# Two tile placements and the place of the second per-layer-embedding products, in a kernel of two blocks

## The chip, the core and the metric

The kernel runs on one core of one Trainium2 chip. The metric is the device time of one execution in microseconds (us); less is better. The engines are named as in the profile: PE (matrix products), DVE, ACT and POOL (vector, scalar and general work), SP (it only issues DMAs here). ACT and POOL issue DMAs as well.

## What is computed

Input is one sequence of T = 512 tokens of width D = 1024, all in fp32. Two blocks follow each other. Cut to what the change touches:

```
# first block, its end: mixture of experts and final norm
x = x + gate1 * (concat(gmlp(h), rwkv7(h)) @ w_out)
h = modulate(rmsnorm(x), shift2, scale2)
group = top1(softmax(h @ rg_w + rg_b)); pick = top2(softmax(logits of its 8 experts))
y = sum over the 2 picked of 32 experts: w * ((silu(h @ w_gate[e]) * (h @ w_up[e])) @ w_down[e])
x = rmsnorm(x + gate2 * y) * final_norm_g
# second block, for i in 0, 1
x = layer_norm(alpha * x + mixer_i(x));  x = layer_norm(alpha * x + swiglu(x))
x = x + (p[i] @ w_ple[i]) * sigmoid(x @ w_ple_gate[i] + b[i])
```

The products `p[i] @ w_ple[i]` (a 512x256 by a 256x1024 matrix for each layer i, "ple products" below) depend on inputs alone, so they can run at any time before layer i ends. They are computed ahead, written to DRAM and read back when the layer needs them.

## The kernel before

**Arithmetic.** Every fp32 product is made of three products in a faster format: each operand is split into a high part and a remainder, and PE computes high x high, high x low and low x high (`mm3`, lines L281 to L283; for the experts `lin`, L1281 to L1283). A weight is loaded as it is into a "raw" tile (`load`, L251, issued by SP), then `conv` makes the high part on ACT (`whi`, L259) and the remainder on DVE (`wlo`, L260). A raw tile can be loaded again once its `wlo` is done, and a pair of parts can be written again once the last product that reads it is done.

**Tiles and order.** Tiles come from pools that are stacked in the on-chip memory in the order in which they are opened. A pool that lies where an older one lay has to wait for the readers of the older tiles. Every engine runs its own instructions in a fixed order that a planner sets from the program text, and waits on semaphores where data or a place isn't ready. `weights` (the function) opens for a stage the pools of low parts, then of raw tiles, then of high parts. In the experts a raw tile or a part is 8 KB of each partition (2048 fp32 values, 1 MB in all); there are five raw tiles and two groups of two pairs of parts, used in turn. Counted in bytes of a partition: `moe` opens a pool at 19,840 with the sorted inputs `xsort`, the constants `c2` and small tiles up to 67,968; the low parts follow up to 100,736, the raw tiles up to 141,696, the high parts up to 174,464. What lay there before: the activation parts of the first block's `w_out` products from 56,704 to 89,472 (read until the last of these products), its own weight tiles below 56,704, and tiles that were done earlier above 89,472.

**Start of the experts (`moe`, L1058).** Early loads: the two halves of expert 0's gate weights (`raw0`), and of layer 0's ple products `pT` and `w_ple` (`rawp`), and then up weights. The router follows (L1099 to L1231): normalisation L1099 to L1104 with L322, L323 and L327, choice of experts on DVE, a count of places on PE (L1202) and DVE (L1201, L1204). The normalised tokens are written to DRAM (`h2d`, L1112) and fetched back in the order of the experts by eight gathers on POOL (`sort`, L1256), turned by PE (L1262) and scaled into `xsort` (L1267, L1269). The ple products of layer 0 stand behind the first gather in the text (L1272); their results leave through ACT (`po`, L1054) and an ACT-issued DMA (L1055). Expert 0 starts with L1281 on `x0h`.

**End of the experts.** `down` of expert 31 ends with `ey` on DVE (L1343) and an adding scatter into `yd` in DRAM, issued by POOL (L1344). Then comes a branch (`tc.If`, L1419) over extra blocks of tokens, which isn't taken here; every engine passes it.

**Start of the second block (`second`).** Weights come in raw tiles of 1024 values (four of them; seven pairs of parts). `ple_load` and `ple_in` fetch and convert pT and w_ple of layer 1; `y` tiles are loaded from `yd` by SP (L1515); `group(2048)` and `group(2304)` load the four raw tiles of `w_mix` that the first products need. `stats` squares y on ACT (L1527), and makes 1/sqrt on ACT and POOL (L1528, L314 to L318); `normed` scales y on DVE (L1535), turns it on PE (L1540) and writes and splits x (L1542, L287, L288). The ple products of layer 1 stand in two parts: five of eight column blocks before the first `normed`, three after the second `stats`. Then 192 products of 256 columns each follow ("bc products", four outputs, eight k, two halves, three products each): the first half with k outside, so that the first steps already want two of the four w_mix tiles, the first and the third. Behind them come x's way to DRAM (`xd`, L1567), the convolution (L1583 to L1587) and the w_dt products (from `s_wdr`, L1601).

## Time and profile before

| | us |
|---|---|
| three runs | 2479.7, 2475.49, 2478.95 |
| median | 2478.95 |
| the profiled execution | 2484.5 |
| its span, first to last instruction | 2482.6 |
| PE busy in it | 2390.5 |
| DVE busy | 1618.2 |
| ACT busy | 1135.6 |
| POOL busy | 231.8 |

All rows come from the one profiled execution, 5.5 us above the median of the runs. Between its span and its own time lie 1.9 us. Of the span, 383 to 467 us is the start of the experts, 467 to 1049 us the experts, and 1049 to 1106 us the way from the last expert through the bc products. In a row of the timeline the columns are start, duration, engine (an engine's name with a q is its queue of issues), line, operation, output<-inputs, shape and count; brackets at the end give the time that the engine stood idle just before, and what it waited for.

### The profile page before, as it was taken

The numbers are of one execution on the slowest core, as the hardware profiler recorded it, in microseconds if no ns is written. First come the engines' busy times: TensorE is split into PE (matmuls) and PEld (weight loads), VectorE is DVE, ScalarE is ACT, GpSimd is POOL, SyncE is SP. The second block draws the span as 40 slices with busy tenths as digits, with TensorE's granted clock in tenths as the row PEclk, the third lists the DMA queues.
The fourth block names the chain that finished last, engine by engine and source line by source line (L and its number), as shares of the span: only waits on it lengthen the run. The fifth ranks groups of instructions, "written<-read, shape, count | busy, mean of one in ns | idle before, by whom it ended". The sixth has DMA issues, their size and how long they took to land.

```text
span 2482.6 us, 36164 instructions
## 1 busy us (share of the span) xinstructions
PE 2390.5 (96%) x14570; PEld 1872.2 (75%) x14570; DVE 1618.2 (65%) x2543; ACT 1135.6 (46%) x1452; POOL 231.8 (9%) x73
## 2 busy tenths in 40 slices
PE   7999999799999999889999999999999998999998
PEld 3788677576666666568878898888888678888887
DVE  4778775699999999866766473333394677333346
ACT  2633324577677777564335333232353654223233
POOL 0000000112334444400000000000000000000000
PEclk9999999899999999989999999999999999999999
DMA  7233334799999999672323323322333112323232
GB/s 250 90 108 109 102 101 176 288 353 354 361 359 359 357 356 359 235 242 86 119 80 113 124 94 102 97 91 92 102 107 107 35 35 86 102 85 109 91 98 69
DMA packets 187307, 408.39 MB, mean 164 GB/s; under 512 B 13408, under 2 KB 130704, under 8 KB 162560
## 3 DMA queue, kind: packets, MB, share of 16 engines
q1 hardware_dynamic: 175840, 383.00, 44.2%
q0 software_dynamic: 5536, 10.46, 1.8%
q10 hardware_dynamic: 5760, 12.59, 1.4%
q8 instruction: 115, 1.88, 0.3%
q14 instruction: 56, 0.46, 0.0%
HBM read 389.17 MB, written 25.21 MB: 167 GB/s over the span
## 4 chain that ended last, share of the span: by engine, by line
PE 52%; DMA 17%; DVE 3%; issue 3%; ACT 1%; POOLq 0%; SPq 0%; DVEq 0%; ACTq 0%
PE mm L282 16%; PE mm L281 16%; PE mm L283 16%; DMA yd<-ey,r 15%; PE sc L1969 1%; PE po L1977 1%; PE pt L1946 1%; DMA raw<-in_w_mix_dram 1%; DVE x L1471 1%; DVE wlo L260 1%; DVE x L1472 0%; DMA s_row<-ard 0%; PE aux L1715 0%; DVE x L1473 0%; DVE xl L288 0%
## 5 line engine op out<-in xcount | busy, mean ns | idle before, releaser
L260 DVE TENSOR_TENSOR wlo<-raw,whi 128x1024 fp32r<-128x1024 f32 (+3 forms) x461 | 756.2, 1652 | 259.5 <-ACT whi L259 258.9
L281 PE MATMUL mm<-xh,whi 128*128 128x512 f32 (+1 forms) x2264 | 833.4, 370 | 17.5 <-ACT xh L287 6.8
L259 ACT ACTIVATE whi<-raw 128x1024 fp32r<-128x1024 f32 (+3 forms) x461 | 637.4, 1403 | 463.2 <-PE mm L282 374.7
L282 PE MATMUL mm<-xl,whi 128*128 128x512 f32 (+1 forms) x2264 | 832.7, 368 | 2.1 <-DVE xl L288 1.8
L283 PE MATMUL mm<-xh,wlo 128*128 128x512 f32 (+1 forms) x2264 | 831.2, 368 | 0.6 <-DVE wlo L260 0.6
L281 PEld LDWEIGHTS mm<-xh,whi 128*128 128x128 f32 x2264 | 427.2, 190 | 96.3 <-issue 9.4
L282 PEld LDWEIGHTS mm<-xl,whi 128*128 128x128 f32 x2264 | 430.3, 190 | 72.5 <-DVE xl L288 4.0
L283 PEld LDWEIGHTS mm<-xh,wlo 128*128 128x128 f32 x2264 | 429.7, 190 | 72.5 <-issue 5.2
L1344 POOL DMA_INDIRECT yd<-ey,r x32 | 210.9, 6590 | 380.7 <-DVE ey L1343 375.8
L1283 PE MATMUL mm<-wlo,exh 128*96 128x512 f32 x496 | 198.0, 401 | 12.1 <-DVE wlo L260 12.0
L1281 PE MATMUL mm<-whi,exh 128*96 128x512 f32 x496 | 197.0, 397 | 4.8 <-ACT exh L287 2.7
L1282 PE MATMUL mm<-whi,exl 128*96 128x512 f32 x496 | 195.8, 395 | 0.0
L1841 DVE TENSOR_TENSOR l_h<-l_sg,mm 128x512 f32<-128x512 f32 x44 | 30.2, 688 | 182.6 <-PE mm L283 167.0
L1283 PEld LDWEIGHTS mm<-wlo,exh 128*96 128x96 f32 x496 | 80.4, 162 | 56.9 <-DVE wlo L260 23.3
L1281 PEld LDWEIGHTS mm<-whi,exh 128*96 128x96 f32 x496 | 80.9, 163 | 38.0 <-ACT whi L259 3.0
L1282 PEld LDWEIGHTS mm<-whi,exl 128*96 128x96 f32 x496 | 80.6, 162 | 35.1
L1282 PE MATMUL aux<-whi,ehl 128*96 128x512 f32 x256 | 100.6, 394 | 0.8 <-DVE ehl L288 0.8
L1281 PE MATMUL aux<-whi,ehh 128*96 128x512 f32 x256 | 100.6, 393 | 0.0
L1283 PE MATMUL aux<-wlo,ehh 128*96 128x512 f32 x256 | 98.4, 400 | 0.0
L287 ACT ACTIVATE xh<-l_h 128x512 fp32r<-128x512 f32 x44 | 27.2, 623 | 111.7 <-DVE l_h L1841 111.7
L1840 ACT ACTIVATE l_sg<-mm 128x512 f32<-128x512 f32 x44 | 25.8, 589 | 83.1 <-PE mm L283 83.0
L1282 PEld LDWEIGHTS aux<-whi,ehl 128*96 128x96 f32 x256 | 41.3, 161 | 19.3 <-DVE ehl L288 1.2
(570 smaller groups left out, 2546.4 us busy)
## 6 DMA issues: line engine op xcount, KB each, us to landing
raw<-in_moe_gate_dram SPq DMA_DIRECT2D x64, 1024.0 KB, 7.5
raw<-in_moe_up_dram SPq DMA_DIRECT2D x64, 1024.0 KB, 7.4
raw<-in_moe_down_dram SPq DMA_DIRECT2D x64, 1024.0 KB, 8.6
raw<-in_w_mix_dram SPq DMA_DIRECT2D x44, 512.0 KB, 3.5
raw<-in_w_ffn_gate_dram SPq DMA_DIRECT2D x44, 512.0 KB, 3.5
raw<-in_w_ffn_up_dram SPq DMA_DIRECT2D x44, 512.0 KB, 3.5
raw<-in_w_ffn_down_dram SPq DMA_DIRECT2D x40, 512.0 KB, 3.3
raw<-in_ada_w_dram SPq DMA_DIRECT2D x64, 256.0 KB, 2.7
```

Source lines behind the costliest of these rows:

```text
L259: nc.scalar.activation(hi[:, :m], r[:, :m], AF.Copy)
L260: nc.vector.tensor_tensor(lo[:, :m], r[:, :m], hi[:, :m], op=OP.subtract)
L281: nc.tensor.matmul(ps, h, xh, start=start, stop=False)
L282: nc.tensor.matmul(ps, h, xl, start=False, stop=False)
L283: nc.tensor.matmul(ps, l, xh, start=False, stop=stop)
L287: self.nc.scalar.activation(xh, src, AF.Copy)
L1281: nc.tensor.matmul(ps, xh[:, k, :], wh, start=(k == 0), stop=False)
L1282: nc.tensor.matmul(ps, xl[:, k, :], wh, start=False, stop=False)
L1283: nc.tensor.matmul(ps, xh[:, k, :], wl, start=False, stop=(k == len(ww) - 1))
L1344: nc.gpsimd.indirect_dma_start(out=yd, out_offset=bass.IndirectOffsetOnAxis(ap=yi, axis=0), in_=y, in_offset=None, bounds_check=T - 1, oob ...
L1840: nc.scalar.activation(sg, pp["g", j], AF.Silu)
L1841: V.tensor_tensor(h, sg, pp["u", j], op=OP.mult)
```

## The change

In `weights` the raw tiles' pool is opened first, ahead of the low parts: it takes 67,968 to 108,928, the low parts move up to 108,928 to 141,696, the high parts stay. A new method `only` restricts the parts to one of the two groups. `conv` can work in pieces of a number of columns; `ple_in` and the first gate weights use pieces of 512. In `moe` the tile `grow` is allocated behind `xsort`, so that `c2` and the small tiles lie 4 KB higher. After `down` of expert 31 and ahead of the branch, pT and w_ple of layer 1 are loaded and converted with the parts of group 0; group 1 is left to the extra blocks. Behind the branch all ple products of layer 1 run in one go, and their results go to eight slices of `xsort`, from where they are written out. In `second` the y loads are issued by POOL, x's tile is allocated behind the y tiles and the statistics' tiles, each half of the statistics has tiles of its own, and the mean and 1/sqrt are made on DVE (and ACT) without POOL.

```diff
     def weights(self, es, raw, hi, lo, wt=WT):
+        self.raw = pool("raw", raw)
         los = [pool("lop", b) for b in lo]
-        self.raw = pool("raw", raw)
         self.groups = [(pool("hip", b), l) for b, l in zip(hi, los)]
         self.hip, self.lop = (sum((g[i] for g in self.groups), []) for i in range(2))
+    def only(self, i):
+        self.hip, self.lop = (list(p) for p in self.groups[i])
...
-    def conv(self, r, kt, n):
+    def conv(self, r, kt, n, step=None):
...
-        nc.scalar.activation(hi[:, :m], r[:, :m], AF.Copy)
-        nc.vector.tensor_tensor(lo[:, :m], r[:, :m], hi[:, :m], op=OP.subtract)
+        for o in range(0, m, step or m):
+            s = slice(o, min(m, o + (step or m)))
+            nc.scalar.activation(hi[:, s], r[:, s], AF.Copy)
+            nc.vector.tensor_tensor(lo[:, s], r[:, s], hi[:, s], op=OP.subtract)
...
-    return K.conv(*raw[0]), sum((K.conv(*r) for r in raw[1:]), [])
-def ple(K, i, ops, bank, room, ms_=range(8)):
+    return K.conv(*raw[0], 512), sum((K.conv(*r, 512) for r in raw[1:]), [])
+def ple(K, i, ops, bank, room):
...
     xsort = mo.tile([128, DC, SLOTS + BLK], F32, name="xsort")
+    grow = mo.tile([128, D], F32, name="grow")
     K.const("c2", mo)
...
     for r in raw0:
-        wg0 += K.conv(*r)
-    grow = mo.tile([128, D], F32, name="grow")
+        wg0 += K.conv(*r, 512)
...
     down(31, *hid, yi[:, 31:], ws[:, 31:])
+    K.only(KEEP)
+    p1 = ple_in(K, ple_load(K, 1))
+    K.only(1 - KEEP)
     total = nc.values_load(nxi[0:1, 0:1], min_val=0, max_val=MORE,
...
     with tc.If(total > 0):
         overflow(total)
+    outs = [xsort[:, m, :T] for m in range(DC)]
+    ple(K, 1, p1, K.mm, lambda: outs.pop(0))
...
-    x = fp.tile([128, DC, T], F32, name="x0")
...
-    p1 = ple_in(K, ple_load(K, 1))
     for b in range(4):
-        nc.sync.dma_start(ys[b], K.yd[b * 128:(b + 1) * 128, :])
+        nc.gpsimd.dma_start(ys[b], K.yd[b * 128:(b + 1) * 128, :])
...
+    nv, nr = ([fp.tile([128, 2], F32, name=f"{n_}{h_}") for h_ in range(2)] for n_ in ("nv", "nr"))
+    sqs = [fp.tile([128, D], BF16, name="sq", bufs=2) for _ in range(4)]
+    x = fp.tile([128, DC, T], F32, name="x0")
...
-        nc.gpsimd.tensor_scalar(v, v, 1.0 / D, 1e-6, op0=OP.mult, op1=OP.add)
-        K.rsqrt(v, r, None, nc.gpsimd)
+        V.tensor_scalar(v, v, 1.0 / D, 1e-6, op0=OP.mult, op1=OP.add)
+        K.rsqrt(v, r)
...
     stats(0)
-    room = lambda: fp.tile([128, T], F32, name="po", bufs=4)
-    ple(K, 1, p1, K.aux, room, range(PM))
     normed(0)
     normed(1)
     stats(1)
-    ple(K, 1, p1, K.aux, room, range(PM, 8))
```

## Rows read from the trace of the kernel before

**Rows 1.** The page's head and its line of PE's busy time (busy us, share of the span, instructions).

```profile
span 2482.6 us, 36164 instructions
PE 2390.5 (96%) x14570; PEld 1872.2 (75%) x14570; DVE 1618.2 (65%) x2543; ACT 1135.6 (46%) x1452; POOL 231.8 (9%) x73
```

**Rows 2.** The view by stretches: stretch in us of the span, its length, busy us and instructions of PE, PE's weight loads, DVE, ACT and POOL, PE's granted clock (1.00 is full), the DMA engines' mean busy share, GB/s. First stretches at the experts' start, then one in their middle, then at their end.

```profile
420.00:425.00 5.00, 2.71 (x20) 2.17 (x19) 5.00 (x8) 2.11 (x7) 0.00 (x0) 1.00 0.50 197
440.00:445.00 5.00, 0.58 (x4) 0.52 (x4) 2.01 (x13) 0.39 (x1) 0.00 (x0) 0.81 1.00 385
445.00:450.00 5.00, 4.74 (x16) 4.26 (x17) 1.50 (x7) 2.00 (x4) 0.00 (x0) 0.50 0.36 136
450.00:455.00 5.00, 5.00 (x27) 4.40 (x27) 3.49 (x21) 0.00 (x0) 2.81 (x3) 0.67 0.60 192
600.00:1000.00 400.00, 387.54 (x1695) 267.76 (x1693) 368.84 (x244) 284.82 (x201) 172.87 (x23) 1.00 0.97 356
1030.00:1040.00 10.00, 10.00 (x47) 7.12 (x46) 8.70 (x6) 6.00 (x4) 3.73 (x1) 1.00 0.09 20
1060.00:1070.00 10.00, 7.11 (x21) 5.50 (x22) 1.93 (x3) 6.93 (x11) 0.97 (x5) 0.61 1.02 363
```

**Rows 3.** The timeline of SP's queue at the experts' start: the first of the early loads, and the constants' load behind them.

```profile
383.58 0.86 SPq L251 DMA_DIRECT2D raw<-in_moe_gate_dram  x2
...
418.23 0.34 SPq L201 DMA_DIRECT2D cst_c<-in_c_dram  x1
```

**Rows 4.** The timeline of DVE at the experts' start: the last eviction of the first block's w_out products, three of the four early `wlo`, and two steps of the router's normalisation.

```profile
419.16 0.75 DVE L902 SCALAR_TENSOR_TENSOR x<-mm,mod,x 128x512 f32<-128x512 f32 x1 [1.96 <-PE mm L283]
419.83 2.28 DVE L260 TENSOR_TENSOR wlo<-raw,whi 128x2048 fp32r<-128x2048 f32 x1
...
423.13 2.29 DVE L260 TENSOR_TENSOR wlo<-raw,whi 128x2048 fp32r<-128x2048 f32 x1
425.33 0.15 DVE L1099 TENSOR_TENSOR n<-sq 128x4 f32<-128x4 f32 x1
...
427.89 2.28 DVE L260 TENSOR_TENSOR wlo<-raw,whi 128x2048 fp32r<-128x2048 f32 x1
430.09 0.15 DVE L327 SCALAR_TENSOR_TENSOR n<-n,n 128x4 f32<-128x4 f32 x1
```

**Rows 5.** The timeline of all engines from the router's end to the first expert.

```profile
441.27 0.58 PE L1202 MATMUL aux<-r,R 128*128 128x8 f32 x4 [1.53 <-DVE r L1198]
...
444.61 0.60 ACT L1054 ACTIVATE po<-mm 128x512 f32<-128x512 f32 x1 [7.45 <-DMA ple<-po]
...
451.58 1.06 POOL L1256 DMA_INDIRECT xt<-h2d,r  x1 [15.14 <-DVE B L1221]
...
466.62 0.65 PE L1281 MATMUL mm<-whi,x0h 128*96 128x512 f32 x1
```

**Rows 6.** The timeline of all engines from the last expert to the bc products (rows of different engines in order of time).

```profile
1048.24 0.39 PE L1283 MATMUL aux<-wlo,ehh 128*96 128x512 f32 x1
1048.67 0.75 DVE L1343 SCALAR_TENSOR_TENSOR ey<-aux,r,grow 96x512 f32<-96x512 f32 x1 [1.09 <-PE aux L1283]
1049.81 0.39 SPq L251 DMA_DIRECT2D raw<-in_pT_dram  x1
...
1051.69 1.42 POOL L1344 DMA_INDIRECT yd<-ey,r  x1 [4.93 <-DMA yd<-ey,r]
...
1056.10 0.79 PE L281 MATMUL aux<-whi 128*128 128x512 f32 x1 [7.47 <-DVE wlo L260]
...
1057.35 2.04 SPq L1515 DMA_DIRECT2D y<-yd  x4
...
1062.89 0.79 PE L281 MATMUL aux<-whi 128*128 128x512 f32 x1 [4.74 <-ACT whi L259]
...
1067.33 0.59 PE L282 MATMUL aux<-wlo,whi 128*128 128x512 f32 x1
...
1069.30 1.42 DVE L1535 TENSOR_SCALAR y<-y,nr 128x1024 f32<-128x1024 f32 x2 [5.20 <-POOL nr L318]
...
1071.43 1.03 PE L1540 MATMUL aux<-cst_c,y 128*128 128x128 f32 x8
```

**Rows 7.** The timeline at the beginning of the bc products (the last two of the four w_mix remainders on DVE, PE's first products) and at their end (PE's last bc product and the first of w_dt).

```profile
1076.14 2.35 DVE L260 TENSOR_TENSOR wlo<-raw,whi 128x1024 fp32r<-128x1024 f32 x2
...
1079.14 0.63 PE L281 MATMUL mm<-xh,whi 128*128 128x256 f32 x4
1080.95 0.39 PE L282 MATMUL mm<-xl,whi 128*128 128x256 f32 x1 [1.18 <-DVE xl L288]
...
1105.21 0.28 PE L283 MATMUL mm<-xh,wlo 128*128 128x256 f32 x1
1106.49 0.41 PE L281 MATMUL mm<-xh,wdh 128*16 128x512 f32 x1 [1.00 <-ACT wdh L287]
```

**Rows 8.** The view of one tile, x, in its stretch: count, duration in ns (min, median, max) of the remainder of 512 columns on DVE.

```profile
L288 DVE TENSOR_TENSOR xl<-x,xh x8: 676/682/684, 1079.0 to 1092.6; 128x512 fp32r<-128x512 f32 x8
```

**Rows 9.** The view of the tile po, which carries the ple results: us from the issue of its DMAs to their landing.

```profile
DMA to landing us min/median/max: 2.0/2.5/9.2
```

**Rows 10.** The view of one line, L1344, the scatter: duration in ns (min, median, max), first and last start in us.

```profile
L1344 POOL DMA_INDIRECT yd<-ey,r x32: 1416/8083/8087, 509.2 to 1051.7; - x32
```

**Rows 11.** The page's list of DMA issues: KB of each, us from issue to landing.

```profile
raw<-in_w_mix_dram SPq DMA_DIRECT2D x44, 512.0 KB, 3.5
```

More of the change, by code (lines that the diff above doesn't have):

```diff
@@ L1024 @@
 RAWR = 2
-PM = 5
+KEEP = 0
 SLOTS = 2 * T
@@ L1040, in ple_in @@
 def ple_in(K, raw):
-    return K.conv(*raw[0]), sum((K.conv(*r) for r in raw[1:]), [])
-def ple(K, i, ops, bank, room, ms_=range(8)):
+    return K.conv(*raw[0], 512), sum((K.conv(*r, 512) for r in raw[1:]), [])
+def ple(K, i, ops, bank, room):
     ps_, wp = ops
-    for m in ms_:
+    for m in range(8):
         ms = slice(m * 128, m * 128 + 128)
@@ L1520, in second @@
     rs = []
+    nv, nr = ([fp.tile([128, 2], F32, name=f"{n_}{h_}") for h_ in range(2)] for n_ in ("nv", "nr"))
+    sqs = [fp.tile([128, D], BF16, name="sq", bufs=2) for _ in range(4)]
+    x = fp.tile([128, DC, T], F32, name="x0")
     def stats(half):
-        v, r = (fp.tile([128, 2], F32, name=n_, bufs=2) for n_ in ("nv", "nr"))
+        v, r = nv[half], nr[half]
         for b in range(2):
-            sq = fp.tile([128, D], BF16, name="sq")
-            nc.scalar.activation(sq, ys[2 * half + b], AF.Square, accum_out=v[:, b:b + 1])
-        nc.gpsimd.tensor_scalar(v, v, 1.0 / D, 1e-6, op0=OP.mult, op1=OP.add)
-        K.rsqrt(v, r, None, nc.gpsimd)
+            nc.scalar.activation(sqs[2 * half + b], ys[2 * half + b], AF.Square, accum_out=v[:, b:b + 1])
+        V.tensor_scalar(v, v, 1.0 / D, 1e-6, op0=OP.mult, op1=OP.add)
+        K.rsqrt(v, r)
         rs.extend((r[:, 0:1], r[:, 1:2]))
```

## The prediction

> **What bounds the kernel now.** I read the views in this order: the head of the page, the stretches, the timelines of the stretches that the change touches, and the rows of single tiles and lines for prices. PE is busy 96% of the span [rows 1], so there is little idle time to win, and the reader's first question is where it lies. In the middle of the experts nothing is to be won: PE is busy 387.5 of 400 us and the DMA engines 0.97 [rows 2], and the change alters nothing there. Two stretches are left, one at each end of the experts.
>
> At the start, PE does 0.58 us of work in 440 to 445 [rows 2], and the first expert begins at 466.62 [rows 5]. What ends last is the router's chain on DVE, then the count on PE, then the gathers (first one issued at 451.58 [rows 5]). Two things stretch this chain. The early `wlo` of 2.28 us each stand between the router's steps [rows 4]. And ACT waits 7.45 us for the DMA of an earlier ple result before it can empty a bank [rows 5], with PE's queue behind it, while the DMA engines are full (share 1.00 [rows 2]). The early raw loads are issued at 383.58, yet the first `wlo` comes at 419.83, right behind the eviction of the last w_out product (419.16, 0.75 us) [rows 3, 4]: the low parts' place is what it waits for. The constants go out only at 418.23 [rows 3] for the same reason.
>
> At the end, the last expert product starts at 1048.24, PE's next is one of layer 1's ple products at 1056.10, and they run on steadily only from 1062.89 [rows 6], because pT and w_ple are asked for at 1049.81, behind the branch. The clock has fallen by then: the granted clock in 1060 to 1070 is 0.61 on average [rows 2]. From 1062.89 to 1067.33 there are eleven products at 0.44 us each [rows 6], the rate of the lower level of 1.2 GHz; in the experts a product takes 387.54/1695 = 0.229 us at full clock, 2.4 GHz [rows 2]. Meanwhile y is fetched (1057.35) and scaled at 1069.30 after a wait for POOL [rows 6], and the bc products start at 1079.14 and run on from 1080.95, held by the split of x, with the w_mix remainders only just done (1076.14 + 2.35 = 1078.5) [rows 7].
>
> **The change part by part. End of the experts.** The two loads of layer 1's ple inputs, 1.5 MB, move into a stretch in which the DMA engines are at 0.09 [rows 2]; at 356 GB/s they take 4.2 us: free. Were that cover gone they would cost these 4.2 us at most. Their conversion is six pieces of 512. The parts of group 0 are those of expert 31's last weights, so the bulk waits for PE's last product, 1048.63. DVE is free of `ey` at 1049.42 [rows 6]; a piece is 0.68 us on DVE [rows 8], and ACT runs a piece ahead, and the first column block wants five of six: 1049.4 + 5 x 0.68 = 1052.8. I add no sum for the branch, since PE passes it while DVE works. The 48 products then take 11 x 0.44 + 37 x 0.229 = 13.3 us if the clock falls as before: 1066.1. Ends: 11.0 us if it doesn't fall (1063.8), 21.1 if it stays low (1073.9).
>
> What is late next is a wait that the change adds. The results are kept in `xsort`, at the lowest addresses, and that is where the raw tiles of the second block begin. Their w_mix loads, issued at 1059.44 now [rows 6], must wait until the ple results have been read out. An eviction and issue is some 0.9 us (0.60 [rows 5] and 0.34 for an issue [rows 3]), a landing 2.0 to 9.2, median 2.5 [rows 9]: 1069.5. Queued behind on SP is all of w_mix, and the bc products wait for that. Four tiles of 0.5 MB follow each other at 0.5 MB / 356 GB/s = 1.47 us; the first lands after 3.5 us [rows 11], the third, which the first bc step wants, 2.9 later: 1076.2 with the issues. Its two conversions at 1.2 each (two took 2.35 [rows 7]) end at 1078.6. Before, the stream ran from 1080.95: 2.6 us gained with the six products that can go ahead, against four now.
>
> The other edits there. The y loads on POOL start when the scatter has landed, as now: nothing. 1/sqrt without POOL saves some 0.7 us of y's way, but y and x are then done ahead of the weights, so this covers itself and gives nothing. The second half's transposes (16, at 1.03 us for eight [rows 6]: 2.1 us) can fill the gap before the weights; I take 1.0, ends 0 and 2.1. The w_dt wait of 1.00 us [rows 7] should go, because its tile no longer lies where x's output is still being read: 1.0, ends 0 and 1.0. Against this, PE now has a gap of up to 12 us before the bc products with only transposes in it. After a gap of 7.5 us the clock was low (above); eleven products at 0.44 in place of 0.229 cost 2.3. I take half, 1.2, ends 0 and 2.3. Sum: 2.6 + 1.0 + 1.0 - 1.2 = 3.4 us gained. Upper end: outputs land 2.3 us sooner, 4.9 + 2.1 + 1.0 = 8. Lower end: low clock all the way through the 48 products, 7.8 us later: 2.6 - 7.8 + 1.0 = -4.2.
>
> One rule of the Trainium skill speaks against one of these edits. The page "SBUF — State Buffer", section "SBUF: two separate sides", says that a DMA issued from POOL needs POOL to write its descriptors, that a DVE operation holding their shared port locks it out, and that such DMAs belong on ACT or SP. The trace agrees in direction: the scatters beside DVE's `wlo` take 8.08 us in the median, the last one, with DVE idle, 1.42 [rows 6, 10]. By it four y loads beside DVE would issue up to 4 x (8.08 - 1.42) = 27 us later; I charge nothing, because no DVE work is due between the pieces' end at 1053.5 and y's scaling.
>
> **Start of the experts.** The raw tiles change places with the low parts. So the conversions are free of the w_out products, but now the raw tiles lie where the w_out activations are read until about 419. I expect the first loads (gate 0, pT, w_ple, the first up weights: 4.5 MB, 12.6 us at 356 GB/s) behind the constants at 419.5 instead of 383.58. Their conversions then arrive between 425 and 437 as pieces of 0.68, in the router's chain or in its gaps, in place of `wlo` of 2.28. Without any `wlo` the chain would win about 5 us: 2.2 before L1099 (423.13 to 425.33) and 3.5 of other `wlo` between L1099 and L327, of which 2.28 is the one shown [rows 4]. But 14 pieces cost 9.5 us if all of them land in the chain. So the chain alone lies between 5 gained and 9.5 - 5.7 = 3.8 lost. The other bound is transfers: up to the gathers the DMA engines idle (1 - 0.50) x 5 + (1 - 0.36) x 5 + (1 - 0.60) x 5 = 7.7 us in 420 to 455 [rows 2], which 12.6 us don't fit into: 4.9 us lost if they all stand in front of the gathers. On the other side, fewer ple products stand in front of the count, and the 7.45 us wait of ACT need not come again. Between these I take zero, ends 10 lost (below) and 5 gained. The moved `grow` and the constants' place 4 KB higher: the constants still wait for the same products, nothing.
>
> The total is 3.4 us. The profiled execution lies 5.5 us above the median; a difference is the same from either, so I take it off the median: 2478.95 - 3.4 = 2475.5, rounded 2475.
>
> **The rivals.** *R1, slower: the late loads collide.* The 4.5 MB delay the gathers by 4.9 us, and w_ple comes last, so that two column blocks' more ple products, 12 at 0.44 = 5.3 us, stand on PE between the gathers and expert 0. Together 10.2 lost, less 3.4 at the end: 2478.95 + 6.8 = 2486. It decides from the point where the first gather is issued later than 451.58 + 4.9 = 456.5. For it: the place argument and the full DMA engines in 440 to 445 [rows 2]. Against it: PE has 4.4 us free there, and gathers need only what DVE's short steps give.
>
> *R2: the change doesn't do what it says at the end.* PE's first ple product comes no earlier than now, 1056.1, because the pieces stand behind the branch or the parts: results land at 1072.8, third weights at 1081.9, 0.9 later than now with 1.0 of w_dt gained and the clock's 1.2 lost: 2480. For it: the parts of group 0 are in use until the last product. Against it: six pieces are short.
>
> *R3: both ends gain.* The early conversions leave the router's chain altogether, because the planner puts them into gaps or some raw tiles' places are free early (those above 89,472): 5 + 3.4 = 8.4, 2470.5. For it: pieces fit into DVE's gaps (DVE works 2.01 of 5 us in 440 to 445 [rows 2]). Against it: the gathers may then wait for transfers.
>
> **How the numbers follow.** Forecast 0.42 (2475, itself from 2470 to 2481), R1 0.17 (2486), R2 0.14 (2480), R3 0.22 (2470), other 0.05. A measurement of this kernel can tell about 0.2%, 5.0 us, from no change: faster means below 2474, slower above 2484. Faster: R3, 0.17 of the forecast and 0.03 of others, 0.42. Slower: R1 and 0.03 of the rest, 0.20. Same: 0.38. The range 2466 to 2487 leaves out the best of R3 with a full clock at the end (8 + 5 gained) and the worst of R1.
>
> **What would show it.** Right: pT and w_ple of layer 1 issued by SP before 1040; PE's first ple product of layer 1 within 5 us of its last expert product; the w_mix loads some 10 us behind where they are now, right after the last ple result has landed; bc products about 3 us sooner, held by a `wlo` of w_mix and no longer by x; no wait before w_dt. At the start: gate 0's loads at about 419.5, pieces of `wlo` from 425 on, expert 0 at 466.6 give or take 5. Wrong: first loads still at 384 (then R3), a first gather after 456.5 (R1), y loads of several us each on POOL (the port), or w_mix loads that don't wait for the ple results (then the end gains several us more).

## The result and the profile after

| | before | after |
|---|---|---|
| median of the runs, us | 2477.74 (5 runs) | 2493.1 (5 runs, 2484.54 to 2494.04) |
| ratio after to before | | 1.0056, 95% interval 1.0042 to 1.007 |
| the profiled execution, us | 2484.5 | 2494.04 |

The change costs 0.56%, some 14 us, where 3.4 us of gain were forecast. One of the five runs of after is 8 us faster than the other four. The head of the page of after, answering [rows 1], says that PE's busy time is nearly the same (2390.5 before): of the 9.6 us by which the span grew, 2.2 are busy time and the rest is idle time:

```profile
span 2492.2 us, 36180 instructions
...
PE 2392.7 (96%) x14570; PEld 1876.5 (75%) x14570; DVE 1619.7 (65%) x2564; ACT 1137.1 (46%) x1465; POOL 249.5 (10%) x67
```

The view by stretches of after, with the columns of [rows 2]:

```profile
440.00:445.00 5.00, 4.98 (x27) 4.71 (x25) 4.01 (x21) 0.00 (x0) 1.90 (x2) 0.50 1.04 420
445.00:450.00 5.00, 3.62 (x15) 3.23 (x16) 4.55 (x18) 0.60 (x1) 3.78 (x5) 0.50 0.96 357
450.00:455.00 5.00, 5.00 (x20) 4.19 (x19) 3.14 (x9) 1.66 (x3) 2.68 (x3) 0.73 1.00 408
...
460.00:465.00 5.00, 1.27 (x3) 1.08 (x4) 0.56 (x1) 1.33 (x2) 0.00 (x0) 0.79 1.02 411
465.00:470.00 5.00, 5.00 (x15) 3.86 (x15) 0.39 (x1) 2.37 (x3) 0.00 (x0) 0.53 0.45 175
470.00:475.00 5.00, 5.00 (x23) 3.48 (x22) 2.91 (x2) 3.77 (x5) 0.00 (x0) 1.00 0.43 116
...
600.00:1000.00 400.00, 388.13 (x1698) 268.45 (x1697) 370.35 (x247) 283.09 (x200) 180.54 (x23) 1.00 0.98 357
```

The middle of the experts is unchanged (last line, against 387.54 in [rows 2]). At the start the picture has turned round. PE is busy in 440 to 445, where it had 0.58 us of work, but at 0.50 of its clock; the DMA engines, which had room in 445 to 455 (0.36, 0.60), are full; and the room has moved to 465 to 475 (0.45, 0.43).

The timeline of after at the experts' start, rows of several engines in order of time, answering [rows 3 to 5]:

```profile
418.73 0.33 SPq L201 DMA_DIRECT2D cst_c<-in_c_dram  x1
419.16 0.85 SPq L255 DMA_DIRECT2D raw<-in_moe_gate_dram  x2
...
422.66 0.16 DVE L1106 TENSOR_TENSOR n<-sq 128x4 f32<-128x4 f32 x1 [0.17 <-ACT sq L1012]
...
442.80 1.03 POOL L1262 DMA_INDIRECT xt<-h2d,r  x1 [12.69 <-DVE B L1228]
...
452.46 20.95 SPq L255 DMA_DIRECT2D raw<-in_moe_up_dram  x2
...
463.07 0.60 ACT L1060 ACTIVATE po<-mm 128x512 f32<-128x512 f32 x1 [5.36 <-DMA ple<-po]
...
463.73 0.79 PE L287 MATMUL mm<-whi 128*128 128x512 f32 x1 [4.11 <-ACT po L1060]
...
469.50 0.58 PE L1287 MATMUL mm<-whi,x0h 128*96 128x512 f32 x1
...
475.71 1.61 PE L1268 MATMUL aux<-cst_c,xt 128*128 128x128 f32 x13
...
492.78 0.47 PE L1287 MATMUL mm<-whi,exh 128*96 128x512 f32 x1 [2.11 <-ACT exh L293]
```

Gate 0's load goes out at 419.16 in place of 383.58. The router is quicker without the large `wlo`: its normalisation starts at 422.66 in place of 425.33, the first gather at 442.80 in place of 451.58. And yet expert 0 begins at 469.50 in place of 466.62. Between them stand an eviction that waits for the DMA of an earlier ple result, twelve ple products at the lower clock (463.73 to 469.0), and on SP's queue a row of 20.95 us, at the end of which the second half of expert 1's up weights is asked for. The last two rows are the turning of gathered rows on PE, which now stands behind expert 0's first product, and the first product of expert 1.

The timeline of after at the experts' end, answering [rows 6, 7]; the last expert product starts at 1053.05:

```profile
1032.86 0.38 SPq L255 DMA_DIRECT2D raw<-in_pT_dram  x1
...
1053.05 0.39 PE L1289 MATMUL aux<-wlo,ehh 128*96 128x512 f32 x1
1053.93 0.50 PE L287 MATMUL mm<-whi 128*128 128x512 f32 x1 [0.49 <-ACT whi L265]
...
1057.06 0.60 ACT L1060 ACTIVATE xsort<-mm 128x512 f32<-128x512 f32 x1 [1.62 <-DVEq L1429]
...
1063.39 2.12 POOL L1524 DMA_DIRECT2D y<-yd  x4 [3.15 <-DMA yd<-ey,r]
...
1067.00 1.06 ACT L1538 ACTIVATE sq<-y 128x1024 bf16<-128x1024 f32 x1 [9.35 <-DMA y<-yd]
...
1068.69 0.80 PE L287 MATMUL mm<-whi 128*128 128x512 f32 x1 [6.39 <-ACT xsort L1060]
...
1075.53 0.60 ACT L1060 ACTIVATE xsort<-mm 128x512 f32<-128x512 f32 x1 [0.79 <-PE mm L289]
...
1076.52 1.28 ACT L326 ACT_TABLE_LOAD   x1 [0.39 <-ACT xsort L1060]
...
1078.29 10.62 SPq L255 DMA_DIRECT2D raw<-in_w_mix_dram  x7
1078.70 1.42 DVE L1546 TENSOR_SCALAR y<-y,nr 128x1024 f32<-128x1024 f32 x2
...
1089.17 0.58 PE L288 MATMUL mm<-xl,whi 128*128 128x256 f32 x1 [1.06 <-DVE xl L294]
...
1115.83 0.40 PE L287 MATMUL mm<-xh,wdh 128*16 128x512 f32 x1
```

The inputs come early and PE's first ple product stands 0.88 us behind the last expert product. But ACT's second eviction stands behind the first square, which waits 9.35 us for y. PE, its four banks full, waits 6.39 us; the last eviction ends at 1076.1, 1/sqrt comes behind it, and w_mix is asked for when the last results have left `xsort`. From the last expert product, y is scaled after 25.65 us (21.06 in [rows 6]), x's low part is first used after 36.12 (32.71 in [rows 7]) and w_dt starts after 62.78 (58.25).

### The profile page after: what moved, and what is told of

It reads as the page before. It is cut to its first block, busy times and chain, and to the rows that moved or that the text cites. A ratio compares the mean times of both kernels' runs of the same rounds, so it can differ in the third digit from the quotient of the medians.

```text
span 2492.2 us, 36180 instructions
## 1 busy us (share of the span) xinstructions
PE 2392.7 (96%) x14570; PEld 1876.5 (75%) x14570; DVE 1619.7 (65%) x2564; ACT 1137.1 (46%) x1465; POOL 249.5 (10%) x67
## 4 chain that ended last, share of the span: by engine, by line
PE 53%; DVE 2%; DMA 1%; ACT 1%; issue 0%; SPq 0%; ACTq 0%; POOLq 0%; DVEq 0%
PE mm L288 16%; PE mm L287 16%; PE mm L289 16%; PE sc L1977 1%; PE po L1985 1%; PE pt L1954 1%; DMA s_row<-ard 0%; DVE x L1483 0%; PE aux L1723 0%; DMA raw<-in_w_mix_dram 0%; PE aux L1725 0%; DMA yd<-ey,r 0%; DVE x L1484 0%; ACT whi L265 0%; DVE wlo L266 0%
## 5 line engine op out<-in xcount | busy, mean ns | idle before, releaser
L1350 POOL DMA_INDIRECT yd<-ey,r x32 | 228.0, 7125 | 377.0 <-DVE ey L1349 361.9
L1849 DVE TENSOR_TENSOR l_h<-l_sg,mm 128x512 f32<-128x512 f32 x44 | 30.1, 687 | 182.5 <-PE mm L289 167.0
L1289 PEld LDWEIGHTS mm<-wlo,exh 128*96 128x96 f32 x496 | 80.6, 162 | 57.2 <-DVE wlo L266 23.8
L1848 ACT ACTIVATE l_sg<-mm 128x512 f32<-128x512 f32 x44 | 25.8, 588 | 83.1 <-PE mm L289 82.9
```

The source lines that it names most:

```text
L1289: nc.tensor.matmul(ps, xh[:, k, :], wl, start=False, stop=(k == len(ww) - 1))
L1350: nc.gpsimd.indirect_dma_start(out=yd, out_offset=bass.IndirectOffsetOnAxis(ap=yi, axis=0), in_=y, in_offset=None, bounds_check=T - 1, oob ...
L1848: nc.scalar.activation(sg, pp["g", j], AF.Silu)
L1849: V.tensor_tensor(h, sg, pp["u", j], op=OP.mult)
```

## The experiments

Two theories, one for each end. *Start*: the raw tiles' new place sends 4.5 MB of loads into a stretch in which the DMA engines are needed for the gathers and the next weights; rivals are the pieces of conversions, the order of the ple products on PE, and the order of conversions. *End*: the evictions on ACT stand in y's way and PE's banks fill; rivals are the results' place, for which w_mix waits, and PE's clock.

All experiments in one table. "Expert 1": from the issue of the constants' load (L201) to the first product of gate and up of expert 1 on DVE. It is the mark for the start, as from there to the same step of expert 31 all nineteen profiles need 530.0 to 534.0 us. "y", "xl" and "w_dt": from the last expert product to y's scaling, the first use of x's low part, and the first w_dt product. The marks come from the one profiled run of each kernel; in e4, s1 and e6 this run lies 9.1, 5.7 and 4.8 us below the median of the timed runs, so there the marks show less than the ratio does.

| kernel | ratio to before, 95% interval | expert 1 | y | xl | w_dt |
|---|---|---|---|---|---|
| before | 1 | 85.6 | 21.1 | 32.7 | 58.3 |
| b1, before again | a single run | 86.8 | 21.0 | 32.5 | 58.8 |
| after | 1.0056, 1.0042 to 1.007 | 91.2 | 25.7 | 36.1 | 62.8 |
| a2, after again | a single run | 91.5 | 25.4 | 35.6 | 62.4 |
| e1, start edits alone | 1.0044, 1.0031 to 1.0057 | 89.8 | 18.9 | 32.5 | 58.2 |
| s1, pools' order alone | 1.0036, 1.0022 to 1.0049 | 90.6 | 19.0 | 32.6 | 58.0 |
| e7, after without the order | 1.0019, 1.0005 to 1.0033 | 86.8 | 25.3 | 35.6 | 62.2 |
| e4, ple behind expert 0 | 1.0097, 1.0084 to 1.011 | 95.7 | 25.8 | 35.3 | 61.0 |
| e8, ple inputs first | 1.0057, 1.0044 to 1.0069 | 91.8 | 25.6 | 35.3 | 61.0 |
| e2, end edits alone | 1.0015, 1.0006 to 1.0023 | 81.9 | 24.7 | 34.9 | 61.5 |
| e6, group 1 for ple | 1.0071, 1.0059 to 1.0083 | 91.8 | 21.8 | 36.0 | 62.4 |
| g1, fewer products | 1.0016, 1.0005 to 1.0026 | 86.5 | 20.2 | 31.4 | 57.9 |
| g2, y from elsewhere | 0.9998, 0.9989 to 1.0007 | 81.9 | 20.7 | 32.5 | 58.0 |
| c1, y loads by POOL | 1.0046, 1.0033 to 1.006 | 80.6 | 30.1 | 39.2 | 65.4 |
| c2, the second block's edits | 0.9998, 0.9989 to 1.0007 | 82.3 | 22.3 | 33.9 | 58.2 |
| d1, e2 and results elsewhere | 1.0044, 1.0031 to 1.0058 | 82.6 | 28.3 | 39.7 | 65.5 |
| d2, d1 and evictions on DVE | 1.0021, 1.0009 to 1.0034 | 82.0 | 22.5 | 34.7 | 61.3 |
| f1, d1 and products ahead | 1.0042, 1.0029 to 1.0055 | 86.2 | 33.4 | 40.9 | 67.4 |
| f2, f1 and y first on SP | 1.0026, 1.0016 to 1.0036 | 86.2 | 22.3 | 36.5 | 62.2 |

**Each end alone.** e1 is before with the pools' order, `grow`'s place and the pieces; e2 is after with those three undone.

> The kernel before with the edits at the experts' start alone (pools' order, place of grow and the constants, pieces of 512 for gate 0 and layer 0's ple inputs); the end is as before. Theory (two separate losses, at the start 12 ple products at the low clock in front of expert 0): the first expert product at about 469.5, the last at about 1053.0, 4.8 us later than before, ratio 1.002. Rival (one loss: the traces of before and after differ at the end only through a shift that the start causes): the whole difference is here, ratio 1.005.

> The changed kernel with the edits at the experts' start undone (pools' order, grow, whole conversions); the end is as changed. Theory: the last expert product at 1048.2 as before; ACT's squares of y stand in front of the second eviction of the ple results, PE stands some 6 us, w_mix is loaded at about 1073.5, the bc products end about 5 us later than before, ratio 1.002. Rival (the end gains the 3 us that were forecast once its start isn't disturbed): ratio 0.999.

e1 1.0044 and e2 1.0015 add up to 1.0059; after has 1.0056. Both ends lose, the start three times as much as the end. For each 1.002 was expected: the end came near it, the start cost twice as much, and e1's first expert product came at 465.67 and not at 469.5. The pools' order stands in `weights`, which the second block calls too, so e1 changes the second block's places and e2 lacks that change: in e1 y is scaled 2.2 us sooner than in before, but xl and w_dt are where they were, so up to there the start's loss is not from the second block.

**Which edit of the start.** s1 is before with one line moved; e7 is after with the same line moved back:

```diff
+        self.raw = pool("raw", raw)
         los = [pool("lop", b) for b in lo]
-        self.raw = pool("raw", raw)
```

> The kernel before with the raw tiles' pool opened first and nothing else of the change (whole conversions, grow in its old place). If the raw tiles' place is what costs at the start, the raw loads go out only behind the constants (about 418 us), and the time is 1.003 to 1.005 of before, as with the start's three edits together (1.0044). If the pieces or the place of grow cost, this kernel stays within 0.1% of before.

> The changed kernel with the order of the pools in weights alone undone (low parts first, raw tiles behind them); pieces of 512 and grow's place stay. Theory (raw tiles that wait for the place of the w_out activations, so that layer 0's ple products come 15 us late): the first loads go out some 35 us ahead of the constants' load again; expert 1's gate times up comes 82 us after the constants' load, give or take 2, in place of 91.2; ratio to before about 1.002. Rival (the pieces in the router's chain and gaps): it stays at 89 to 91, ratio 1.005.

The order alone takes 1.0036 of the 1.0044, and without it after falls to 1.0019, not to be told from e2 (1.0015). e7's mark came at 86.8 and not at the expected 82; the kernels with the start of before that ran on the same chip (b1, g1, f1, f2) have 86.2 to 86.8. So the pieces and `grow` cost nothing that can be measured, and the order of the pools is the cause of the loss at the start. The order moves the raw tiles and the low parts; no run separates the two, and that it is the raw tiles' place which costs is read from the timeline. In s1, which has none of the other edits, SP's queue shows the loads behind the constants, as in after:

```profile
413.65 0.33 SPq L201 DMA_DIRECT2D cst_c<-in_c_dram  x1
414.57 0.81 SPq L251 DMA_DIRECT2D raw<-in_moe_gate_dram  x2
...
447.11 21.63 SPq L251 DMA_DIRECT2D raw<-in_moe_up_dram  x2
```

The gathers then take longer. The list of DMA issues in 440 to 480 gives the count of the last four gathers and the median us from issue to landing; after, then before:

```profile
ht<-h2d,r POOLq DMA_INDIRECT x4, 14.7
...
ht<-h2d,r POOLq DMA_INDIRECT x4, 6.5
```

In s1 the median is 10.8; in c2 6.5. In before no raw load is issued between 437.19 and 467.52, around the gathers; in after three are, from 446.68 to 452.46, among them. The last gather of after is issued 8.7 us sooner (33.6 us behind the constants' load in place of 42.3), takes 8.0 longer (14.5 in place of 6.5) and lands 0.8 sooner (48.1, 48.9). So the landing itself doesn't make expert 1 late. Nor does the second half of expert 1's up weights: it lands 59.5 us behind the constants' load, in before 59.3. What is late is the turning of the rows on PE. The rows of before:

```profile
463.70 3.28 PE L1262 MATMUL aux<-cst_c,xt 128*128 128x128 f32 x14 [1.37 <-ACT grow L1247]
...
487.35 0.65 PE L1281 MATMUL mm<-whi,exh 128*96 128x512 f32 x1 [2.71 <-ACT exh L287]
```

Expert 1's first product waits for its x in both kernels, and x for the last turned rows. In before two of the 32 turning products of the first four gathers stand behind expert 0's first product, in after 21; the last of all 64 starts 65.7 us behind the constants' load in before and 70.8 in after, and expert 1's first product at 69.1 and 74.1. From that product of after PE's rows lead back, with no stop of more than 2.11 us, to the ple product at 463.73, which waits for an eviction, which waits for the landing of an earlier ple result.

**The order of work around expert 0.** e4 is after with layer 0's ple products behind expert 0's gate and up; e8 is after with the ple inputs converted ahead of expert 0's gate weights.

```diff
-    ple(K, 0, p0, K.mm, lambda: mo.tile([128, T], F32, name="po", bufs=2))
...
     g = gated(0, None, rt.tile([BLK, 512], F32, name="eg0"), wg0)
+    ple(K, 0, p0, K.mm, lambda: mo.tile([128, T], F32, name="po", bufs=2))
```

> The changed kernel with layer 0's ple products moved in the text behind expert 0's gate and up products. Theory (PE's queue: 12 ple products that wait for ACT, which waits for a landing, stand in front of expert 0): the first expert product comes at 458 to 462 in place of 469.5, the last expert product 5 to 8 us earlier than in the changed kernel, 1045 to 1048; ratio to before about 1.002 to 1.003. Rival (transfers: 4.5 MB too late for a loop that is bound by DMA): the last expert product stays at 1053, ratio 1.005.

> The changed kernel with layer 0's ple inputs converted ahead of gate 0's weights (two statements exchanged); loads stay late. Theory (order of DVE's pieces and of PE's queue: 12 ple products, and behind them the conversion of gate 1, which takes the parts that they free, stand in front of the first experts): expert 1's gate times up comes 84 to 87 us after the constants' load, ratio about 1.003. Rival (late transfers alone): it stays at 90 or more, ratio 1.005.

Expert 0's first product comes 14.5 us sooner in e4 (36.25 us behind the constants' load in place of 50.77), and expert 1 still comes 4.5 later; e8 changes nothing (91.8 against 91.2). So bringing expert 0 forward doesn't help, and the theory that I had for both runs failed; e4 is even 0.97% slower than before. But neither run takes the ple products off the way to expert 1. In e4 42 of the 48 stand behind expert 0's products and ahead of the last turned rows, and ACT waits for the landing of a ple result with the rows' evictions behind it, and PE for these:

```profile
487.05 0.60 ACT L1060 ACTIVATE po<-mm 128x512 f32<-128x512 f32 x1 [4.46 <-DMA ple<-po]
...
489.26 1.12 PE L1268 MATMUL aux<-cst_c,ht 128*128 128x128 f32 x4 [7.50 <-ACT xsort L1273]
```

In e8 PE has started the last of the 48 at 37.2 us behind the constants' load, and then ACT's order holds the turned rows up:

```profile
458.15 0.60 ACT L1060 ACTIVATE po<-mm 128x512 f32<-128x512 f32 x1 [9.04 <-DMA ple<-po]
```

That layer 0's ple results, late as a whole, are what expert 1 waits for is a rival that both timelines fit. No run left them out.

**Group 1 for the ple products.** e6 is after with `KEEP = 1`: the parts of expert 31's other weights, which lie where y's tiles will be.

> The changed kernel with one constant changed: layer 1's ple inputs take the parts of group 1 in place of group 0. Then the y tiles lie where these parts are read until the last ple product, the planner puts all eight evictions in front of the squares on ACT, and y is asked for only after the products. Theory (ACT's order: squares that wait for y in front of the evictions): PE runs the 48 products without the stop of 6.4 us, at full clock, to about 1065; w_mix is asked for at about 1068 in place of 1078.3; the bc products run from about 1082 in place of 1089; 6 to 8 us faster than the changed kernel, ratio to before about 1.002. Rival (the wait of w_mix for the results in xsort costs the time in any order, and y is later now): no gain on the changed kernel, ratio 1.005 or more.

Here all evictions stand ahead of the squares on ACT, PE runs its 48 products at full clock without a stop, and w_mix is asked for 16.9 us behind the last expert product in place of 25.2. And w_dt comes no sooner (62.4), and the ratio is 1.0071: the y loads now wait for PE's last ple product, PE then stands idle and its granted clock falls to 0.50, and DVE does the w_mix remainders ahead of x. The mechanism that I had named was there, its gain was not.

**Are the ple products on the path?** g1 is before with one product in place of six for each column block of layer 1.

```diff
+        if i:
+            K.nc.tensor.matmul(ps, wp[0][0][:, ms], ps_[0][0], start=True, stop=True)
+        else:
...
```

> The kernel before with one product of six for each column block of layer 1's ple result (40 of 48 products are left out; loads, evictions and writes stay). Theory (y's way from the last scatter sets the bc products, and the ple products only fill the wait): the bc products start within 1.5 us of 32.7 us after the last expert product, ratio 0.9995 to 1.0005, and perhaps slower where PE's clock falls in the gap. Rival (the forecast's reading, that the ple products stand on the path): they start 5 to 9 us sooner, ratio 0.997.

> The kernel before, unchanged, for a second profile of it. Theory (its first profile was of an execution with a slow start of the experts): counted from the issue of the constants' load, expert 0's first product at 45 us and expert 1's gate times up at 82, as in the run with the end alone changed, where this code is the same; span about 2476. Rival: 48.4 and 85.6 as in the first profile, and the run with the end alone owes its start to something in its code.

40 products less, 9.2 us of PE's time at 0.229 each, move w_dt by 0.9 us against b1 (57.9, 58.8), and the runs are 0.16% slower. This loss lies behind the mark: from w_dt to the end g1's profile needs 1382.3 us and b1's 1378.4. In before the products fill a wait that is there anyway. b1 has the start of before's first profile again (86.8), and not the 82 that was expected.

**What that wait is.** g2 is before with y fetched from `h2d`, c1 is before with the y loads on POOL, c2 is before with all the edits in `second` that leave the ple products alone.

```diff
-    K.yd = yd
+    K.yd = h2d
```

> The kernel before with y fetched from the table h2d, which is complete long before, in place of the experts' sum yd; so the output is another one, and y no longer waits for the last scatter. If the way from the last scatter through y binds the start of the bc products, they come 5 to 8 us sooner, time 0.997 to 0.998. If the ple products or the w_mix remainders bind it, bc moves by less than 2 us.

> The kernel before with the y loads issued by POOL in place of SP, and nothing else. If the w_mix loads are late in before because they stand behind the y loads in SP's queue, which wait for the last scatter, w_mix is asked for within about 4 us of the last expert product in place of 11.2, and the bc products (30.9 us behind the last expert product in before) come up to 3 us sooner, bound by x's split then; time 0.9985 to 0.9995. If y's own chain binds them, or the raw tiles are taken by the ple inputs, bc moves by less than 1 us and the time is the same.

> The kernel before with those edits of the second block that leave the ple products where they are: y loads by POOL, x's tile behind the y tiles, own tiles for each half of the statistics, 1/sqrt without POOL. If y's chain binds the bc products once w_mix is early, this one scales y 1 to 2 us sooner than the kernel with the y loads alone and starts bc as much sooner: 0.998 to 0.9995. If the evictions of the ple products on ACT delay 1/sqrt, as in the changed kernel, y is scaled no sooner and the time is that of the y loads alone, 0.999 to 1.0005.

g2 didn't do what I meant. The timeline of SP's queue in it, with the last expert product at 1041.01:

```profile
1043.03 7.51 SPq L251 DMA_DIRECT2D raw<-in_w_ple_dram  x2
1050.65 1.85 SPq L1515 DMA_DIRECT2D y<-h2d  x4
```

The second load of w_ple stands in front of y, and the view of SP's waits puts 6.2 us of its wait to the last scatter into `yd`: its place is not free before. So y isn't early, and the run says only that the last scatter holds SP's queue by two ways. c1 missed on the slow side: 1.0046. With y on POOL, w_mix no longer queues behind y, its loads (1053.34) go out beside the y loads (1053.29), and five conversions of weights stand between the first two squares and 1/sqrt on ACT: y is scaled 30.1 us behind. c2, which takes POOL out of 1/sqrt and lays x elsewhere, gets another order from the planner, and is as fast as before.

**The end, taken apart.** d1 is e2 with the results in two low parts of group 1 in place of `xsort`; d2 also evicts on DVE.

```diff
-    outs = [xsort[:, m, :T] for m in range(DC)]
+    pos = [K.wtile(K.lop, F32, "wlo") for _ in range(2)]
+    outs = [p[:, j * T:(j + 1) * T] for p in pos for j in range(4)]
```

> The kernel with the end edits alone, and the ple results kept in the two low parts of group 1 in place of xsort. If the results' place is what costs at the end, w_mix is asked for some 10 us behind the last expert product (24.3 with the results in xsort) and the bc products come 2 to 4 us sooner than there: 0.9985 to 1.000 of before, in place of 1.0015. If the order on ACT costs (the last square and 1/sqrt behind evictions), w_mix is early but bc's first use of x's low part stays at 33 us or later, and the time at 1.001 to 1.002.

> As the one before, and the eight evictions of layer 1's ple products made by DVE in place of ACT (their DMAs stay on ACT). If the order on ACT is what costs, PE's wait of 6.4 us among the ple products goes or shrinks to under 2 us, y is scaled at or before 22 us behind the last expert product in place of 24.7, and the time is 0.1% or more below the kernel without this edit. If it is the results' place alone, this one takes as long as that kernel, within 0.1%.

> The changed kernel again, one look. If a profile of it stands for the timed runs, expert 1's gate times up comes 91.2 us behind the constants' load again, within 1 us, and the bc products 36 us behind the last expert product. If traces of one kernel differ, one of the two moves by 2 us or more.

a2 has after's marks again, within 0.6 us. d1 is worse than e2, and than both its expectations (1.0044 against 1.0015), though w_mix is asked for 4.0 us behind the last expert product. In its timeline, with that product at 1043.52:

```profile
1047.49 39.99 SPq L255 DMA_DIRECT2D raw<-in_w_mix_dram  x11
1055.27 2.25 POOL L1525 DMA_DIRECT2D y<-yd  x4 [6.62 <-DMA yd<-ey,r]
1060.76 1.06 ACT L1539 ACTIVATE sq<-y 128x1024 bf16<-128x1024 f32 x1 [12.65 <-DMA y<-yd]
1062.45 0.79 PE L287 MATMUL mm<-whi 128*128 128x512 f32 x1 [9.66 <-ACT wlo L1060]
1071.86 1.48 DVE L1547 TENSOR_SCALAR y<-y,nr 128x1024 f32<-128x1024 f32 x2
```

With w_mix on the DMA engines, y is there 17.2 us behind the last product in place of 14.0 in after, and all that stands behind the square (PE's stop of 9.66 us, evictions, 1/sqrt) comes later still. So taking away the added wait that the prediction dwelt on wins nothing: the loads that it held back now stand in y's way. d2 wins 0.23% of d1 back: y is scaled at 22.5, 1/sqrt no longer behind the evictions. But PE still stops, now because DVE's order has the same fault:

```profile
1064.66 0.17 DVE L1543 TENSOR_SCALAR nv<-nv 128x2 f32<-128x2 f32 x1 [13.10 <-ACT sq L1542]
...
1065.48 0.79 PE L287 MATMUL mm<-whi 128*128 128x512 f32 x1 [9.20 <-DVE wlo L1061]
```

**Products ahead of the branch.** f1 is d1 with the ple products moved ahead of the branch, so that evictions stand ahead of the squares on ACT; f2 also has the y loads on SP, ahead of w_mix.

```diff
+    pos = [K.wtile(K.lop, F32, "wlo") for _ in range(2)]
+    outs = [p[:, j * T:(j + 1) * T] for p in pos for j in range(4)]
+    ple(K, 1, p1, K.mm, lambda: outs.pop(0))
     total = nc.values_load(nxi[0:1, 0:1], min_val=0, max_val=MORE,
```

> The end edits alone with the results in the low parts of group 1, and the ple products of layer 1 with their evictions moved from behind the branch to ahead of it. So the evictions stand ahead of the squares on ACT. If that order is what costs, PE runs the 48 products without a stop of over 2 us, and y is scaled at most 22 us behind the last expert product (28.3 with the products behind the branch); the time falls from 1.0044 to 1.001 or less. If w_mix taking the DMA engines ahead of y is what costs, y is scaled at 24 us or later and the time stays above 1.002.

> As the one before, with the y loads issued by SP ahead of the w_mix loads, as before the change. If y's way from the last scatter is what binds the stretch, and all that can stand in it has been taken out, y is scaled 17 to 19 us behind the last expert product (21.1 in the kernel before) and the w_dt products come 2 to 3 us sooner than the 58.3 of before: 0.9985 to 0.9995 of before. If PE's clock, low after an idle stretch, takes that back, y is as early but w_dt is at 58 or later and the time is 0.9995 to 1.001.

Both missed their better case. Timeline of f1, the last expert product at 1047.01:

```profile
1063.08 2.16 POOL L1525 DMA_DIRECT2D y<-yd  x4
1072.59 1.06 ACT L1539 ACTIVATE sq<-y 128x1024 bf16<-128x1024 f32 x1 [6.82 <-DMA y<-yd]
1081.24 3.68 PE L1552 MATMUL aux<-cst_c,y 128*128 128x128 f32 x16 [22.18 <-DVE y L1547]
```

PE's stops among the ple products are gone, but what follows the branch is asked for only 13.9 (w_mix) and 16.1 us (y) behind the last expert product, on POOL behind a load that waits for the ple results; y lands 25.6 us behind it; and PE stands still for 22.18 us. In f2 y is scaled at 22.3, and now w_mix, asked for at 15.8, is late: its remainders stand on DVE ahead of x's, xl 36.5. Of the kernels tried none beats before; c2 equals it.

## Why the prediction was wrong, step by step

**The start, "between these I take zero": the term that failed most.** On the chip it is 0.44% (e1), 10.9 us, with 0.36% from the pools' order alone (s1). The loss lies at the end that I had set from the transfers ("10 lost"). My mistake was to let the router's gain stand against it. The gain is real, and larger than my 5: the first gather is issued 9.3 us sooner. It buys nothing. The DMA engines are full from 420 to 465, the next raw loads go out among the gathers and no longer ahead of them, and the last rows land 48.1 us behind the constants' load in place of 48.9. And the ple products, whose inputs come 35 us later, no longer fill PE's waits for the router: in before 42 of the 48 are started when the first gather is issued, in after four. The others stand between the router and expert 1, and the step "the 7.45 us wait of ACT need not come again" failed with them: it came as 5.36 us at 463.07, behind the gathers' issue and no longer ahead of it. I had asked whether 12.6 us of transfers fit in front of the gathers, and not what they push behind them.

**R1** had the right place and nearly the price (10.2 us lost at the start), with a deciding point that was wrong: a first gather after 456.5. It came at 442.80. And its second half, the ple products in front of expert 0, was there to the number (twelve at 0.43 us). Whether it costs what I said is not shown: e4 only moves the products from in front of expert 0 to in front of expert 1. That R1's 10.2 us lie so near the 10.9 of e1 is in part luck, since the gathers were not late.

**The end, "an eviction and issue is some 0.9 us".** That is the price of the instruction; the step held no queue. The evictions are on ACT, whose order puts a square ahead of seven of them, and the square waits for y. So the 48 products take 21.6 us (1053.93 to 1075.5) in place of the 13.3 that I gave them, w_mix is asked for 25.2 us behind the last expert product in place of some 21, and 1/sqrt stands behind the last eviction. "y and x are then done ahead of the weights" failed by the same: y is scaled 4.6 us later than before. The end lost 0.15% (e2, 3.7 us) where 3.4 us of gain were forecast; the lower end of my sum was -4.2, which left out the 2.3 us of low clock that I had named as an end. Both lower ends together, 14.2 us, are nearly the measured loss; I had left them out of the range together, and the steps behind them were others, so this is luck.

**The premise of the end**, that the late ple products hold the bc products, was the deeper fault: the rows of before show them running "steadily only from 1062.89" and I took the visible wait for the bound. g1 shows that they could nearly all be left out. What the runs point to is two ways side by side, nearly of one length: the way from the last scatter through y's load, square and 1/sqrt to x's parts, and w_mix's load and conversion. A shorter first one wins nothing: e1 and s1 scale y 2 us sooner than before (18.9, 19.0), and xl and w_dt stay, since x's low parts stand on DVE behind w_mix's remainders (in s1 1076.78 behind 1075.04). d1 and c1 (w_mix early, y late), e6, f1 and f2 (evictions early; y, x or w_mix late) lengthen one or the other.

**Right:** gate 0's loads at 419.5 (419.16); pT and w_ple before 1040 (1032.86, 1035.06); the first ple product within 5 us (0.88); w_mix waiting for the last result; no wait before w_dt; y's four loads on POOL at no cost of their own (2.12 us for all, with DVE idle). On the last one bears the Trainium skill, page "SBUF — State Buffer", section "SBUF: two separate sides", by which DVE's use of a shared port holds up DMAs issued from POOL: no DVE operation ran beside these four, so the run neither bears it out nor speaks against it. The prediction took the scatters of before for a clearer case than they are: two of 1.42 us (at 577.73 and 684.86) have a `wlo` beside them for 1.0 and 0.7 us. The low clock cost what its upper end said: the bc products from 1089.17 to about 1094.2 run at one per 0.213 us, later ones at 0.12, some 23 of them, 2.2 us.

**Do the traces carry the loss?** The profiles of before and after differ by 5.6 us at expert 1 and by 4.5 at w_dt, 10.1 of some 14. The start code of before shows two values at expert 1: 85.6 to 86.8 in before, b1, g1, f1 and f2, and 80.6 to 82.6 in e2, c1, c2, g2, d1 and d2. b1, g1, f1 and f2 ran on one chip, on which the kernel before took 2482.1 and 2482.7 us in the median; the six others ran on two more chips, on which it took 2477.3 to 2479.0. On one of these two ran a2 and five of the six: a2's 91.5 at expert 1 is 9.5 later than their middle, and its 62.4 at w_dt is 4.3 later than the 58.0 and 58.2 of g2 and c2, which are as fast as before. Together this is 13.8 us, or 0.56%. So the traces of one chip carry the loss, though a2's own time, a single run, is only 11.9 us above the median of before there. Why the first profile of before has the larger value, and lies 5.5 us above the median of its runs, is not shown. The larger value alone doesn't do it, as f1 and f2 have it and don't lie above theirs; and the time up to the constants' load alone differs, from 413.8 to 418.7 us, between profiles with the same code up to there (f2, c1).

**Open:** what expert 1 would win without layer 0's ple results in ACT's and PE's order. That they bind it in after is read from its rows and not shown by a run; e4 and e8 only exclude that the order of ple and expert 0 on PE, or the order of conversions, is all. Also open is which of the two moved pools costs, and why one start code has two values, beyond that they go with the chip in all profiles but that of before, whose chip is not on record.

## What to carry to other kernels

When a tile changes its place, look at which loads its old place had let run ahead under other work; a load moved into a full stretch delays what shares the DMA engines with it there, and the work that waits for it loses the gap that it had filled; a chain that got shorter on the engines didn't pay that back here. An experiment that moves work out of the way of one mark tests it only if the work doesn't come to stand in the way of the next, as in e4. Before taking work out of a gap, find what the gap waits for: if a load or a reduction behind it sets the end, the work in it was free. And an eviction costs what its engine's queue has in front of it; where several inputs meet, as y, w_mix and the results here, bringing one of them forward through the same DMA engines and the same ACT makes another one late.

## What was not expected of the hardware

The last four gathers of after, issued some 9 us sooner than in before but among three raw loads, took 14.7 us in the median to land in place of 6.5, and the last landed only 0.8 us sooner. Fewer products went with a slower kernel: g1, with 40 of 48 left out, has a mean granted clock of 0.980 to 0.984 in its runs, where those of before on the same chip have 0.984 to 0.988, and 0.16% more time; in 1100 to 1150, around and behind the start of w_dt, the granted clock is 0.93 in g1's profile and 0.97 in b1's. After PE's stops of 6.39 us (after) and 9.66 us (d1) the next 12 and 9 products came at some 0.43 us each in place of 0.23, the rate of the lower level of the clock, 1.2 GHz.
